# Inverse norms of a delta rule's keys computed apart from those of its queries

## Chip, core and metric

The kernel runs on one core of a Trainium2 chip. A core has five engines that each work through a queue of their own in order: TensorE (PE in the profile, with its weight loads as PEld), VectorE (DVE), ScalarE (ACT), GpSimd (POOL) and SyncE (SP), which here issues nearly all DMA transfers. Semaphores tie the queues together. The metric is device time in microseconds (us), as the median of several runs.

## What is computed

One layer of a hybrid decoder trunk, with 1024 tokens behind 16 meta tokens, width 1024, float32 in and out. A combined input projection feeds two head groups: a gated delta rule (4 heads, key and value width 128) and a forgetting attention (8 heads). Their outputs go through an output projection, then a SwiGLU network, and a last normalisation. The change concerns the delta rule's front, of which this is the part that matters:

```python
def l2norm(x):
    return x * lax.rsqrt(jnp.sum(x * x, axis=-1, keepdims=True) + EPS)

qkv = jax.nn.silu(causal_dwconv(qkv, conv_w))
q, k, v = jnp.split(qkv, ...)
q = l2norm(q) * (GDN_DK ** -0.5)          # per token and head
k = l2norm(k)
# chunks: a_mat = strict(k k^T * decay * beta), qk = q k^T * decay, then
# (I + a_mat) is inverted per chunk and the state is carried from chunk to chunk
```

So each token and head needs two inverse norms: one of its key and one of its query. Keys' inverse norms enter the matrices `a_mat` and `qk` and the keys that update the state; queries' inverse norms scale only the final output of a chunk.

## The kernel before

The kernel runs through stages: normalisation of the input; gates; the delta rule's projections and its preparation per head; the remaining projections (`z`, `fv`, `fk`, `fq`, lines L203 and L615 to L654 among them); the chunk scan; attention; output projection; the SwiGLU network (L1359) and its down projection (L1522). Large products are split into three float32r products.

Heads are prepared in two pairs. For each pair the code projects and convolves keys, queries and values of two heads (`conv_silu`, products at L193 to L195), then calls `gdn_pre` for each head, then `invert_blocks` (L529, L531), a long row of small VectorE instructions on the tile `up` that inverts 32x32 diagonal blocks for both heads together. The second pair's preparation runs beside the first pair's inversion and beside the `z` and `fv` projections on TensorE.

`gdn_pre(h, kq, vt)` does this, in source order:

- L442: fill `stat` with ones. Its columns 0 to 7 (`NT` = 8 token tiles) will hold the sums of squares of the keys, column 8 that of the 16 meta keys, columns 9 to 16 those of the queries (`NS` = 9).
- L445 to L448: transpose the keys (`tr_k`), copy them to `ktok`, square them on ScalarE into `sq`, reduce on VectorE.
- L449 to L454: transpose the meta keys and values (`trm`), copy to `mkv`, square with a sum.
- L455 to L457: transpose the queries (`tr_q`, in two halves), square on ScalarE, reduce on VectorE.
- L458: add EPS to all 18 columns of `stat` in one VectorE instruction.
- L459, L460: two powers of -1/2 on GpSimd, `rk` (keys) and `rq` (queries).
- L461 to L470: transpose `rk` on TensorE (`prk`, L462 and L463), copy to `rkt` (L465, L466), store to DRAM (`rk_d`, L467 and L468), and read it back spread over all partitions as `rkr` (L470).
- L472, L473, L503, L520: small VectorE products with `rk`.
- L477 to L483: load `gc_d` into `gce`, form the decays (L478 and L479 on VectorE, the exponential L480 on ScalarE, two masks L481 and L483 on GpSimd).
- L489 to L496: products of keys with keys and queries (`pq`), and VectorE instructions that multiply them with the decays and with `nbr` or `rk`.
- L498: multiply `na` with `rkr` on GpSimd; L500 stores its diagonal blocks to `ad_d`, which `invert_blocks` reads (L539).
- L504 (GpSimd, `ktok` times `kf`), L507 (values), L509 to L514 (stores to `rec_d`), L517 to L522 (the meta chunk; L518 multiplies `ems` with `rkr`).

`rq` is read again only at L572, behind all heads, and then in the scan. The tiles that `gdn_pre` transposes into come from a pool of three PSUM banks (`ps_t`).

The result of `invert_blocks` goes to DRAM (L549) and is read back as `ubk` (L597) in `levels`, which copies it on ScalarE and VectorE (L606). The gate tiles `zt` are made at L297 (ScalarE) and L298 (GpSimd) and stored at L299.

The order of the queues is not written by hand here. The source is traced in program order, and the framework's scheduler orders each engine's queue at compile time against its own estimate of how long things take:

```python
with tile.TileContext(nc, schedule_with_timeline_sim=True) as tc:
```

Only TensorE has a hand-written order, from the `z` projection on (`peo.enter_context(tc.manual_schedule(...))`); the second pair's TensorE instructions were written ahead of that and stand among them. Once compiled, every queue is fixed.

Of the kernel before, what the change touches and what calls it, by code (L numbers as in the profile page):

```python
# [12 lines left out]
ALU = mybir.AluOpType  # L13
# [8 lines left out]
NT = S // P  # L22
# [5 lines left out]
EPS = 1e-6  # L28
# [69 lines left out]
def tile_hymba_layer(ctx, tc, x, meta, attn_norm_w, w_in, conv_w, a_log, dt_bias, gdn_norm_w,  # L98
                     fgate_b, w_out, ffn_norm_w, w_gate, w_up, w_down, final_norm_w, out):
    nc = tc.nc  # L100
# [20 lines left out]
    def ps_t(name):  # L121
        return bank("tp", 3, name)
# [15 lines left out]
    mhalf = const.tile([P, 32], F32, name="mhalf")  # L138
# [194 lines left out]
    NS = NT + 1  # L333
# [77 lines left out]
    rk = gpool.tile([P, GH, NS], F32, name="rk")  # L411
# [15 lines left out]
    def tr8(src, nm):  # L427
        pts = []
        for g in range(2):
            pt = ps_t(f"tr_{nm}_{g}")  # L430
            for i in range(4):
                c = NM + P * (4 * g + i)
                nc.tensor.transpose(pt[:, P * i:P * i + P], src[:, c:c + P], ident)
            pts.append(pt)
        return pts

    def v3(ap, n=NT):
        return ap.rearrange("p (t c) -> p t c", t=n)

    def gdn_pre(h, kq, vt):  # L440
        stat = gp.tile([P, 2 * NS], F32, tag="kst", bufs=2, name=f"kst_{h}")
# [10 lines left out]
        mkv = gp.tile([NM, 2, P], F32, tag="mkv", bufs=2, name=f"mkv_{h}")  # L452
        nc.scalar.copy(mkv, pt[:NM, 0:2 * P].rearrange("p (a c) -> p a c", a=2))
        nc.scalar.activation(sqq[:NM, :P], mkv[:, 0], AF.Square, accum_out=stat[:NM, NT:NT + 1])  # L454
        for g, pt in enumerate(tr8(kq[:, 1], f"q{h}")):  # L455
            nc.scalar.activation(sqq[:, 512 * g:512 * g + 512], pt, AF.Square)
        nc.vector.tensor_reduce(stat[:, NS:NS + NT], v3(sqq), AX.X, ALU.add)  # L457
        nc.vector.tensor_scalar(stat, stat, EPS, None, op0=ALU.add)  # L458
        nc.gpsimd.tensor_tensor(rk[:, h], stat[:, 0:NS], mhalf[:, :NS], op=ALU.pow)  # L459
        nc.gpsimd.tensor_tensor(rq[:, h], stat[:, NS:NS + NT], mhalf[:, :NT], op=ALU.pow)  # L460
        prk = ps_t(f"prk_{h}")  # L461
        nc.tensor.transpose(prk[:NT, :P], rk[:, h, 0:NT], ident)  # L462
# [22 lines left out]
        for g in range(4):  # L485
# [6 lines left out]
            for i in range(2):  # L492
                t = 2 * g + i
                nc.vector.scalar_tensor_tensor(na[:, t], pqv[:, i, 0], nbr[:, t:t + 1], na[:, t],
                                               op0=ALU.mult, op1=ALU.mult)
                nc.vector.scalar_tensor_tensor(e[:, t], pqv[:, i, 1], rk[:, h, t:t + 1], e[:, t],  # L496
                                               op0=ALU.mult, op1=ALU.mult)
# [53 lines left out]
    for hp in range(2):  # L551
        c = 2 * P * hp
        kqs = [gp.tile([P, 2, T], F32, tag="kq", bufs=3, name=f"kq_{2 * hp + i}") for i in range(2)]
        vts = [gp.tile([P, T], F32, tag="vt", bufs=2, name=f"vt_{2 * hp + i}") for i in range(2)]
        with ExitStack() as es:
            for ins in (xlds[-1], *casts[6]) if not hp else ():
                es.enter_context(tc.issue_after(ins.ins))
            w = win_block(GK + c, 256, f"gk{hp}")
        for i in range(2):
            conv_silu(w, P * i, 4 + 2 * hp + i, kqs[i][:, 0], f"k{hp}{i}")  # L560
        w = win_block(GQ + c, 256, f"gq{hp}")
        for i in range(2):
            conv_silu(w, P * i, 2 * hp + i, kqs[i][:, 1], f"q{hp}{i}")
        w = win_block(GV + c, 256, f"gv{hp}")
        for i in range(2):
            conv_silu(w, P * i, 8 + 2 * hp + i, vts[i], f"v{hp}{i}")
        for i in range(2):
            gdn_pre(2 * hp + i, kqs[i], vts[i])
        invert_blocks(hp)
# [1067 lines left out]
```

## Time and profile before

| what | value |
|---|---|
| median of 3 runs | 1328.59 us (1327.1 to 1329.35) |
| profiled execution, its own time | 1324.81 us |
| its span in the trace | 1323.1 us |
| instructions | 20046 |
| mean granted TensorE clock | 0.997 |
| stage of `gdn_pre` and `invert_blocks`, heads 0 to 3 | about 116 to 272 us of the span |

The profile's page gives busy time per engine over the span; the waits view sums, for an engine, its idle time by what ended it; the timeline lists instructions one by one with start, length and the idle time before them; the windows view gives busy time of each engine and the granted TensorE clock in chosen stretches. "Granted clock" is the share of full speed that the throttle let TensorE have. A SPq row is the issue of a DMA on SyncE's queue, not the transfer.

### The profile page before, as it was taken

What the parts mean: (1) busy time and instruction counts of PE and PEld (TensorE: products, weight loads), DVE (VectorE), ACT (ScalarE), POOL (GpSimd) and SP (SyncE); (2) the same over time, 40 slices, a digit from 0 to 9 for tenths busy, and PEclk for the clock granted to TensorE, in tenths of its full rate; (3) what the DMA queues carried; (4) which work ended last, traced back from release to release, by engine and by line L of the source; (5) the groups of instructions that cost most, each with busy time, mean ns of one, the idle gap of its engine ahead of it and who ended that gap; (6) DMA issues with size and microseconds to landing.
All of it is one profiled execution on the core that took longest, in us unless ns stands there. A gap on an engine that the chain in (4) does not pass through costs nothing.

```text
span 1323.1 us, 20046 instructions
## 1 busy us (share of the span) xinstructions
PE 1296.6 (98%) x7442; PEld 1133.5 (86%) x7442; DVE 851.8 (64%) x1523; ACT 546.3 (41%) x916; POOL 389.3 (29%) x348
## 2 busy tenths in 40 slices
PE   9999999999999999999899999999999999999997
PEld 8999999899999988877687888888888888888886
DVE  6665789676236588885787665566566565355644
ACT  6543534232223367884553333333333243343332
POOL 2211423501023311113422644553334453010301
PEclk9999999999999999999999999999999999999999
DMA  6331743874479596646544555434444557955513
GB/s 228 98 112 33 213 133 117 221 209 146 147 254 332 180 248 184 165 110 211 171 144 134 192 176 183 151 137 159 159 162 157 175 195 259 408 180 185 213 63 127
DMA packets 184776, 233.88 MB, mean 177 GB/s; under 512 B 19120, under 2 KB 136872, under 8 KB 181864
## 3 DMA queue, kind: packets, MB, share of 16 engines
q1 hardware_dynamic: 181704, 223.70, 52.4%
q0 software_dynamic: 2976, 8.92, 2.2%
q8 instruction: 58, 0.95, 0.3%
q14 instruction: 38, 0.31, 0.1%
HBM read 154.91 MB, written 77.67 MB: 176 GB/s over the span
## 4 chain that ended last, share of the span: by engine, by line
PE 82%; DMA 6%; DVE 5%; issue 3%; POOL 2%; ACT 1%; SPq 1%; POOLq 0%; DVEq 0%; ACTq 0%
PE xp L1522 8%; PE yp L1522 7%; PE gb L1359 5%; PE ud L1359 5%; PE gd L1359 5%; PE ub L1359 5%; PE ua L1359 4%; PE ga L1359 4%; PE pj_fk L203 4%; PE pj_fq L203 4%; PE pt L1005 2%; PE ue L1359 2%; PE ge L1359 2%; PE fv L203 2%; PE wog L203 2%
## 5 line engine op out<-in xcount | busy, mean ns | idle before, releaser
L164 DVE TENSOR_TENSOR al_p<-ra_p,ah_p 128x2048 fp32r<-128x2048 f32 (+1 forms) x21 | 46.7, 2222 | 94.0 <-ACT ah_p L163 94.0
L163 ACT CAST ah_p<-ra_p 128x2048 fp32r<-128x2048 f32 (+1 forms) x21 | 37.1, 1766 | 105.8 <-PE xp L1522 48.5
L1522 PE MATMUL xp<-wh_p,ah_p 128*128 128x512 f32 (+1 forms) x187 | 70.5, 377 | 0.7 <-DVE hs L1549 0.7
L1522 PE MATMUL xp<-wl_p,ah_p 128*128 128x512 f32 (+1 forms) x187 | 70.4, 376 | 0.0
L1522 PE MATMUL xp<-wh_p,al_p 128*128 128x512 f32 (+1 forms) x187 | 70.4, 376 | 0.0
L1412 POOL TENSOR_TENSOR gzw<-gzw,uzt 128x512 f32<-128x512 f32 x11 | 18.4, 1675 | 154.0 <-DVE uzt L1403 127.9
L1412 POOL TENSOR_TENSOR gxy<-gxy,uxy 128x512 f32<-128x512 f32 x22 | 38.7, 1758 | 67.0 <-DVE uxy L1403 48.0
L1359 PE MATMUL gb<-uh_p,w_g_p 128*128 128x512 f32 x176 | 57.8, 389 | 0.0
L1359 PE MATMUL ub<-uh_p,w_u_p 128*128 128x512 f32 x176 | 57.8, 389 | 0.0
L1359 PE MATMUL gd<-uh_p,w_g_p 128*128 128x512 f32 x176 | 57.8, 389 | 0.0
L1359 PE MATMUL ud<-uh_p,w_u_p 128*128 128x512 f32 x176 | 57.8, 389 | 0.0
L979 ACT ACTIVATE pr<-pr,sm 128x144 f32<-128x144 f32 (+3 forms) x64 | 50.6, 792 | 16.5 <-DVE sm L974 16.2
L164 DVE TENSOR_TENSOR w_u_p<-raw_u,w_u_p 128x512 fp32r<-128x512 f32 x42 | 43.2, 1028 | 21.4 <-ACT w_u_p L163 21.3
L164 DVE TENSOR_TENSOR pl<-pt,ph 128x512 fp32r<-128x512 f32 (+1 forms) x96 | 51.4, 553 | 4.6 <-ACT ph L163 3.7
L163 ACT CAST ph<-pt 128x512 fp32r<-128x512 f32 (+1 forms) x96 | 45.4, 474 | 17.8 <-PE pt L1005 17.0
L1359 PE MATMUL ga<-uh_p,w_g_p 128*128 128x512 f32 x160 | 52.5, 389 | 0.0
L1359 PE MATMUL ua<-uh_p,w_u_p 128*128 128x512 f32 x160 | 52.5, 389 | 0.0
L1522 PE MATMUL yp<-wh_p,ah_p 128*128 128x512 f32 x132 | 51.3, 389 | 0.0
L1522 PE MATMUL yp<-wl_p,ah_p 128*128 128x512 f32 x132 | 51.3, 389 | 0.0
L1522 PE MATMUL yp<-wh_p,al_p 128*128 128x512 f32 x132 | 51.3, 389 | 0.0
L164 DVE TENSOR_TENSOR wl_p<-rw_p,wh_p 128x2048 fp32r<-128x2048 f32 (+1 forms) x21 | 46.9, 2235 | 3.4 <-ACT wh_p L163 3.4
L1005 PE MATMUL pt<-ident,pr 128*128 128x128 f32 x288 | 48.1, 276 | 0.0
(638 smaller groups left out, 4265.4 us busy)
## 6 DMA issues: line engine op xcount, KB each, us to landing
ra_p<-ao_p SPq DMA_DIRECT2D x14, 1024.0 KB
raw_g<-in_w_gate_dram SPq DMA_DIRECT2D x22, 512.0 KB
raw_u<-in_w_up_dram SPq DMA_DIRECT2D x22, 512.0 KB
raw_d<-in_w_down_dram SPq DMA_DIRECT2D x22, 512.0 KB
wt_p<-raw_d SPq DMA_DIRECT2D x33, 256.0 KB
rw_p<-wt_p SPq DMA_DIRECT2D x8, 1024.0 KB
rw_p<-in_w_down_dram SPq DMA_DIRECT2D x6, 1024.0 KB
ao_p<-gzw SPq DMA_DIRECT2D x22, 256.0 KB
```

The costliest lines, as they stand in the source:

```text
L163: cast = nc.scalar.copy(dst_hi, src)
L164: tail[0] = (cast, nc.vector.tensor_sub(dst_lo, src, dst_hi.bitcast(F32)))
L203: nc.tensor.matmul(dst, a, b, start=first, stop=last)
L979: nc.scalar.activation(pr[:, :n], pr[:, :n], AF.Exp, bias=sm[:, np_ - 1:np_], scale=-1.0, accum_out=rsum[:, h, j:j + 1])
L1005: nc.tensor.transpose(pt[:rows_k, P * j:P * j + P], pts[j][0][:, c0:c0 + rows_k], ident)
L1359: nc.tensor.matmul(dst, a[:, c], b[:, k], start=(first and k == 0 and i == 0), stop=(k == 3 and i == 2), skip_group_check=not first)
L1412: last_mul[0] = G.tensor_tensor(gs[d], gs[d], us[d], op=ALU.mult)
L1522: nc.tensor.matmul(dst[:, n_], a[:, f, c], b[:, f, n_], start=(first and i == 0 and n == 0), stop=(i == NF - 1 and n == 2), skip_group_che ...
```

## The change

In `gdn_pre` the addition of EPS is split in two: columns of the keys (with the meta keys) and columns of the queries. The keys' addition and the keys' power are placed directly behind the meta keys' squares, in front of the queries' transposes and squares. The queries' addition and power stay where they were. The values are the same; the unused column 17 of `stat` no longer gets EPS.

```diff
         nc.scalar.activation(sqq[:NM, :P], mkv[:, 0], AF.Square, accum_out=stat[:NM, NT:NT + 1])
+        nc.vector.tensor_scalar(stat[:, 0:NS], stat[:, 0:NS], EPS, None, op0=ALU.add)
+        nc.gpsimd.tensor_tensor(rk[:, h], stat[:, 0:NS], mhalf[:, :NS], op=ALU.pow)
         for g, pt in enumerate(tr8(kq[:, 1], f"q{h}")):
             nc.scalar.activation(sqq[:, 512 * g:512 * g + 512], pt, AF.Square)
         nc.vector.tensor_reduce(stat[:, NS:NS + NT], v3(sqq), AX.X, ALU.add)
-        nc.vector.tensor_scalar(stat, stat, EPS, None, op0=ALU.add)
-        nc.gpsimd.tensor_tensor(rk[:, h], stat[:, 0:NS], mhalf[:, :NS], op=ALU.pow)
+        nc.vector.tensor_scalar(stat[:, NS:NS + NT], stat[:, NS:NS + NT], EPS, None, op0=ALU.add)
         nc.gpsimd.tensor_tensor(rq[:, h], stat[:, NS:NS + NT], mhalf[:, :NT], op=ALU.pow)
```

## The prediction

> **What bounds the kernel now.** The page comes first: how full is the busiest engine?
>
> ```profile
> PE 1296.6 (98%) x7442; PEld 1133.5 (86%) x7442; DVE 851.8 (64%) x1523; ACT 546.3 (41%) x916; POOL 389.3 (29%) x348
> ```
>
> TensorE has work in 1296.6 of 1323.1 us, so only its idle 26.5 us, and time at a lowered clock, can be won. Next the waits view, cut to TensorE from 110 to 290 us, the stage around the change (engine, line, what it waited for: us, times, longest):
>
> ```profile
> PE prk L462 <- POOL rk L459: 2.1, 1, 2.1
> PE fv L203 <- DVE up L531: 1.1, 1, 1.1
> PE pq L489 <- DVE gce L496: 0.5, 1, 0.5
> PE tr_q L433 <- ACT mkv L453: 0.3, 1, 0.3
> PE pj_v L193 <- ACT cx_q L419: 0.3, 1, 0.3
> ```
>
> The longest is for the very tile that the change moves: the transposes of `rk` (L462) wait 2.1 us for POOL's power (L459), once in four heads. The timeline shows which head (start, length, instruction, idle time before it):
>
> ```profile
> 239.63 0.27 PE L462 MATMUL prk<-ident,rk 128*8 128x128 f32 x1 [2.13 <-POOL rk L459]
> 237.79 1.79 POOL L459 TENSOR_TENSOR rk<-kst,mhalf 128x9 f32<-128x9 f32 x1 [4.20 <-DVE kst L458]
> ```
>
> It is head 3. The windows view, 1 us each, shows what follows (stretch, length, busy time and count of PE, PEld, DVE, ACT, POOL, then granted clock):
>
> ```profile
> 237.00:238.00 1.00, 0.51 (x5) 0.18 (x2) 1.00 (x3) 0.32 (x1) 0.21 (x1) 1.00 0.98 326
> 238.00:239.00 1.00, 0.00 (x0) 0.00 (x0) 1.00 (x2) 0.00 (x0) 1.00 (x1) 1.00 0.15 51
> 239.00:240.00 1.00, 0.36 (x3) 0.21 (x3) 1.00 (x2) 0.54 (x1) 1.00 (x2) 0.90 0.42 56
> 240.00:241.00 1.00, 1.00 (x6) 1.00 (x6) 1.00 (x5) 1.00 (x1) 1.00 (x1) 0.50 0.51 66
> 241.00:242.00 1.00, 1.00 (x7) 1.00 (x6) 1.00 (x2) 1.00 (x3) 1.00 (x1) 0.50 0.51 68
> 242.00:243.00 1.00, 1.00 (x6) 1.00 (x6) 1.00 (x3) 0.58 (x2) 1.00 (x2) 0.50 0.49 63
> 243.00:244.00 1.00, 1.00 (x10) 1.00 (x9) 0.78 (x3) 0.00 (x0) 1.00 (x2) 0.89 0.08 9
> ```
>
> TensorE counts as full from 240, but its clock is halved: 6 or 7 matmuls per us, where the us at 243 has 10. The lost clock is 0.10 + 3 x 0.50 + 0.11 = 1.71 us. The stall costs 2.13 + 1.71 = 3.84 us.
>
> **Why head 3 is late.** VectorE and ScalarE for this head:
>
> ```profile
> 228.03 1.22 DVE L448 TENSOR_REDUCE kst<-sq 128x8 f32<-128x1024 f32 x1 [1.68 <-ACT sq L447]
> 229.17 0.57 DVE L531 TENSOR_REDUCE up<-up 128x14 f32<-128x406 f32 x1
> 229.65 2.10 DVE L518 TENSOR_TENSOR ems<-ems,rkr 16x16 f32<-16x16 f32 x1
> 234.68 1.21 DVE L457 TENSOR_REDUCE kst<-sq 128x8 f32<-128x1024 f32 x1
> 237.54 0.17 DVE L458 TENSOR_SCALAR kst<-kst 128x18 f32<-128x18 f32 x1
> 238.21 1.21 DVE L479 SCALAR_TENSOR_TENSOR gce<-gce 128x1024 f32<-128x1024 f32 x1
> 228.50 0.18 ACT L454 ACTIVATION_READ_ACCUMULATOR sq<-mkv 16x1 f32 x1
> ```
>
> The sums of the keys are complete at 229.25 (L448) and 228.68 (L454), yet the addition of EPS (L458) runs at 237.54, since it takes keys and queries in one instruction and the queries' sums (L457) stand behind other work. That is 8.3 us between the keys' sums and the instruction that uses them.
>
> **The change, part by part.**
>
> 1. Splitting L458. The rows of the two lines over all four heads:
>
> ```profile
> L458 DVE TENSOR_SCALAR kst<-kst x4: 167/168/175, 125.4 to 237.5; 128x18 f32<-128x18 f32 x4
> L459 POOL TENSOR_TENSOR rk<-kst,mhalf x4: 1794/1802/1887, 125.8 to 237.8; 128x9 f32<-128x9 f32 x4
> ```
>
> Four more VectorE instructions of about 0.17 us each: 0.7 us on an engine busy for 64%. I cost them at nothing, because TensorE's stream covers them; uncovered they cost 0.7 us. POOL's powers are the same four and four; nothing is added there, and no DMA is added or taken away.
>
> 2. The keys' addition and power move ahead. POOL at that time:
>
> ```profile
> 229.32 2.40 POOL L498 TENSOR_TENSOR ktna<-ktna,rkr 128x1024 f32<-128x1024 f32 x1 [5.59 <-DVE kst L448]
> 231.66 1.93 POOL L298 TENSOR_TENSOR zt<-zt,gnw 128x256 f32<-128x256 f32 x2
> ```
>
> The addition can run behind L531 at 229.7, or behind L518 at 231.75. The power follows either at once (229.9 to 231.7), or behind L498 (231.7 to 233.5), or last behind both L298 as well (233.6 to 235.4). Against 239.58 now, `rk` is 4.2 to 7.9 us earlier. I take 233.5, behind L498, since head 2's product stands ahead of head 3's power in the source too. L298 then starts 1.8 us later; it feeds a store of the gate that nothing in this stage reads.
>
> 3. TensorE's place for the transposes. If TensorE kept its place (it comes there at 237.5), the stall would be gone: -3.84. But the queues are ordered at compile time against a model of the times, so the transposes will stand earlier too. What the lag can be is shown by the other heads:
>
> ```profile
> 130.90 0.27 PE L462 MATMUL prk<-ident,rk 128*8 128x128 f32 x1
> 125.79 1.81 POOL L459 TENSOR_TENSOR rk<-kst,mhalf 128x9 f32<-128x9 f32 x1
> 215.30 0.27 PE L462 MATMUL prk<-ident,rk 128*8 128x128 f32 x1
> 213.36 1.89 POOL L459 TENSOR_TENSOR rk<-kst,mhalf 128x9 f32<-128x9 f32 x1 [2.19 <-DVE kst L458]
> ```
>
> Head 0 transposes 3.3 us after its power ends (127.60), head 2 just after it (215.25), head 3 stalls. So a new stall between 0 and 2.1 us is what the rows allow. Head 3 differs by what lay on the queries' path: L518 took 2.10 us there (0.17 at 253.47, below) while L498 ran, and it and the steps behind it leave the path. So I take +0.4 us, without loss of clock: gaps of a µs keep it (270 to 272, below).
>
> [...]
>
> 4. What is late next. TensorE would reach its next stall 3.4 us sooner. That is the wait of `fv` at 272:
>
> ```profile
> 272.01 0.36 PE L203 MATMUL fv<-whi_fv,uh 128*128 128x256 f32 x1 [1.12 <-DVE up L531]
> 270.00:272.00 2.00, 0.89 (x8) 0.51 (x7) 1.92 (x8) 1.93 (x4) 0.00 (x0) 1.00 1.17 297
> 269.80 0.62 ACT L606 COPY u<-ubk 32x512 f32<-32x512 f32 x1 [7.14 <-DMA ubk<-ud_d]
> 255.84 2.40 POOL L498 TENSOR_TENSOR ktna<-ktna,rkr 128x1024 f32<-128x1024 f32 x1 [6.49 <-DVE ktna L494]
> 253.47 0.17 DVE L518 TENSOR_TENSOR ems<-ems,rkr 16x16 f32<-16x16 f32 x1 [2.29 <-DMA rkr<-rk_d]
> 246.34 1.20 SPq L470 DMA_DIRECT2D rkr<-rk_d  x1
> 244.44 0.28 SPq L467 DMA_DIRECT2D rk_d<-rkt  x1
> 238.32 3.79 SPq L549 DMA_DIRECT2D ud_d<-up  x8
> ```
>
> Read upwards: `rkt` is stored at 244.44, read back from 246.34, and VectorE waits 2.29 us for it at 253.47; then POOL's L498, SP's stores and loads of the diagonal blocks, and only then ScalarE's L606, in front of which no `fv` bank is evicted. This chain begins at `rk` too. With `rk` 6 us earlier VectorE's 2.29 goes, and POOL has 1.79 us less ahead of head 3's masks: about 4.1 us sooner, against TensorE's 3.4. So the stall of 1.12 us stays nearly as it is: nothing. Bounds: it vanishes, -1.1, or SP's order keeps the chain where it is and the gain is eaten here.
>
> 5. Heads 0 to 2. Each `rk` comes sooner as well, but TensorE is full there apart from 0.5 + 0.3 + 0.3 us in the waits above: nothing, with -1.1 as a bound.
>
> **Sum.** -2.13 - 1.71 + 0.4 + 0 = -3.4 us. The profiled execution took 1324.81 (span 1323.1 and 1.7 around it); it becomes 1321.4. It is 3.8 below the median of the runs, 1328.59, and I put the same difference on that: 1325.2. With everything favourable: -3.84 - 1.1 - 1.1 = -6.0, 1322.6.
>
> **The rivals.**
>
> *The gain is given back at `fv`.* If the chain of part 4 stays put, TensorE stands there for 1.1 + 3.8 = 4.9 us and restarts at half clock for another 1.7: 1328.6 to 1330.3. If the chain comes 2 us sooner: -2 + 1.7, 1328.3. For it: SP issues in order, and the eight stores of the inversion (L549, until 242.1, the last row above) may stand ahead of the read-back. Against it: VectorE's wait at 253.47 is for `rk` alone.
>
> *The wait moves along with the transposes, and is longer there: slower.* Place: head 3, on TensorE, behind the queries' transposes at about 229. POOL's L498 must wait for its DMA until 229.32, so a power queued behind it ends at 233.5. The queries' transposes end at 229:
>
> ```profile
> 228.31 0.66 PE L433 MATMUL tr_q<-ident,kq 128*128 128x128 f32 x4 [0.28 <-ACT mkv L453]
> ```
>
> If TensorE comes to L462 at 230, it idles 3.5 us, not 2.1; at 228.7, 4.8 us. With the same 1.7 of clock that is +1.4 to +2.7: 1330.0 to 1331.3. It decides from the point at which TensorE comes more than 2.1 us before the power's end. Against it: in three heads of four it came behind.
>
> *The clock is not won back.* [...] If the halved clock at 240 has another cause than the gap of 2.13 us, 1.71 drops out: -2.13 + 0.4 = -1.7, 1326.9. The windows speak against it: the clock falls inside the gap and nowhere else near, though 1.12 us at 272 cost nothing.
>
> [...]
>
> *The change doesn't do what it says.* If the addition or the power is queued as late as now, 1328.6.
>
> **Chances.** A measurement of this kernel tells about 0.2% (2.7 us) from no change. Forecast 0.50 (faster 0.46, same 0.04); given back at `fv` 0.16 (0.02 faster, 0.11 same, 0.03 slower); the wait moves and grows 0.17 (0.02 same, 0.15 slower); the clock stays lost 0.05 (same); VectorE held up 0.02 (same); no effect 0.10 (0.02 faster, 0.07 same, 0.01 slower). Sums: faster 0.50, same 0.31, slower 0.19. The range goes from the favourable sum, 1322.6, to 1331.3, the far end of the slower rival; the forecast's own is 1322.6 to 1327.
>
> **What would show it.** Right: in head 3 `rk` starts by 234 and far ahead of L457; no idle time of 2 us before L462; clock 1.00 from 236 to 246; the second `rkr` of the pair issued by 243; a stall of about 1 us for `fv` near 268. Wrong: a gap of 2 us before L462 at an earlier time with half clock behind it, a gap of 3 us or more before `fv`, or L459 still behind L457.

## The result, and the profile after

The changed kernel takes 1340.09 us (median of 4 runs, 1339.09 to 1341.11); before, beside it, 1327.84 us (4 runs, 1326.06 to 1329.35). The ratio is 1.0095, interval 1.0073 to 1.0117: **slower by 0.95%**, where 0.25% faster was forecast, and outside the range. Timed again later on another occasion, 6 runs gave 1339.01 us against 1330.68, ratio 1.006 (1.0038 to 1.0082). The profiled execution took 1341.11 us, its span is 1339.0. Ratios here and below leave out two single executions that took far longer: one of e9's at 4532.11 us, which e9's median in the table counts, and one of before's at 2592.77 us, beside e5 to e8.

Line numbers of the changed kernel are one higher than before's behind the moved lines: the keys' addition and power are L455 and L456, the transposes of `rk` L463 and L464, `rkt` L466 and L467, `rkr` L471.

The page's busy times come first:

```profile
PE 1305.1 (97%) x7442; PEld 1139.3 (85%) x7442; DVE 850.7 (64%) x1527; ACT 548.4 (41%) x918; POOL 391.8 (29%) x348
```

TensorE has the same 7442 instructions but is busy 8.5 us longer (1296.6 before): it did the same work at a lower clock, 0.992 granted on average against 0.997. Its idle time grew as well. The waits view of TensorE from 110 to 345 us (engine, line, what it waited for: us, times, longest):

```profile
PE prk L463 <- POOL rk L456: 3.0, 3, 1.8
PE pq L490 <- DVE gce L497: 1.8, 1, 1.8
PE pj_v L193 <- ACT cx_q L419: 1.7, 1, 1.7
PE py L641 <- DVE u L631: 1.2, 1, 1.2
PE fv_-1_3081 L203 <- DVE up L532: 0.7, 1, 0.7
PE py L643 <- DVE u L631: 0.6, 1, 0.6
PE fv L203 <- DVE up L532: 0.4, 1, 0.4
PE trm L451 <- ACT vt L425: 0.3, 1, 0.3
```

That is 9.7 us in eight rows; before it was 4.3 in five. The wait for `rk` that the change was to remove is still the largest. It is now spread over three places instead of one, and `cx_q`, `py` and a second `fv` have come in, none of which is a wait for `rk`.

Where was the most lost? The windows view, 3 us each, of the levels behind the heads (length, busy time and count of PE, PEld, DVE, ACT, POOL, granted clock):

```profile
315.00:318.00 3.00, 2.27 (x18) 1.93 (x14) 2.61 (x7) 1.70 (x3) 0.00 (x0) 1.00 0.05 16
318.00:321.00 3.00, 1.91 (x23) 1.59 (x24) 2.87 (x7) 0.58 (x1) 0.00 (x0) 0.95 0.02 5
321.00:324.00 3.00, 3.00 (x17) 2.39 (x15) 0.59 (x2) 0.58 (x1) 0.09 (x1) 0.50 0.35 121
...
333.00:336.00 3.00, 3.00 (x12) 3.00 (x12) 0.52 (x1) 0.41 (x1) 0.97 (x1) 0.50 0.38 126
336.00:339.00 3.00, 3.00 (x16) 3.00 (x15) 0.00 (x0) 0.00 (x1) 0.00 (x0) 0.71 0.34 112
```

TensorE is idle for 0.73 + 1.09 us, and then runs for 17 us at half clock (five whole windows at 0.50 and parts of two): 0.15 + 7.50 + 0.87 = 8.5 us of clock. The same place in before has no such gap, nor have the windows behind it:

```profile
311.00:314.00 3.00, 3.00 (x30) 2.53 (x29) 2.51 (x6) 1.63 (x4) 0.00 (x0) 1.00 0.27 82
```

The timeline names the cause of that gap. After:

```profile
315.27 0.71 DVE L601 STREAM_TRANSPOSE tb<-ubk 128x512 f32<-128x512 f32 x1 [4.11 <-DMA ubk<-ud_d]
...
317.76 0.67 DVE L631 COPY u<-pu 32x512 f32<-32x512 f32 x1
318.49 0.41 PE L641 MATMUL py<-ident,u 64*64 64x64 f32 x4 [1.22 <-DVE u L631]
```

VectorE stood for 4.11 us at the second pair's transposition (it waits for that pair's `ubk`), while the first pair's copies (L631) stood behind it; the last matmul that they wait for ended at 315.2. Before, the two had the other order:

```profile
310.44 1.40 DVE L630 COPY u<-pu 32x512 f32<-32x512 f32 x2 [1.31 <-PE pu L626]
312.54 0.71 DVE L600 STREAM_TRANSPOSE tb<-ubk 128x512 f32<-128x512 f32 x1 [0.40 <-DMA ubk<-ud_d]
```

Nothing in the diff touches this place. The scheduler put VectorE's queue into another order there, and not only there: the tables of queue order that e5, e10 and e12 (below) carry hold another instruction at 452 places of TensorE's queue, 309 of VectorE's, 97 of SP's, 44 of ScalarE's and 23 of POOL's, from the heads to the levels.

The ledger closes up to the scan. The scan behind the levels starts, in the tile view of `sc` (min, median and longest ns, first and last start):

```profile
L971 PE MATMUL sc<-ka,qa x112: 230/368/447, 458.4 to 592.7; 70*128 70x264 f32 x16, 70*128 70x328 f32 x16, 70*128 70x392 f32 x16, 70*128 70x456 f32 x16
```

and after the change

```profile
L972 PE MATMUL sc<-ka,qa x112: 230/368/448, 472.4 to 607.0; 70*128 70x264 f32 x16, 70*128 70x328 f32 x16, 70*128 70x392 f32 x16, 70*128 70x456 f32 x16
```

It starts 14.0 us later, of the 15.9 by which the span grew. More idle time, 9.7 - 4.3 = 5.4, and 8.5 of clock in the levels are 13.9. The half clock behind head 3 (1.7 in the prediction) went, and as much came back behind the wait for `pq` at 248 (0.75, 0.50 and 0.89 in the three stretches of 2 us from 248).

Not every execution loses its clock at the same place. Each run states the mean granted clock of its span, so (1 - clock) x span is the time it lost to the clock. Before loses 4.0 to 4.5 us on average, with 1325.3 to 1326.0 left; the changed kernel lost 11.7 (first 4 runs) and 9.1 (6 runs later), with 1328.4 and 1330.0 left. So of its loss some 6 us are clock and some 4 us idle time. In the profile of the second occasion the levels kept their clock (0.6 us of waits for `u`), and 2.5 us of waiting for `fv` at 268 and others cost it instead.

### The profile page after: what moved, and what is told of

It reads as the page before. It is cut to its first block, busy times and chain, and to the rows that moved or that the text cites. A ratio compares the mean times of both kernels' runs of the same rounds, so it can differ in the third digit from the quotient of the medians.

```text
span 1339.0 us, 20058 instructions
## 1 busy us (share of the span) xinstructions
PE 1305.1 (97%) x7442; PEld 1139.3 (85%) x7442; DVE 850.7 (64%) x1527; ACT 548.4 (41%) x918; POOL 391.8 (29%) x348
## 4 chain that ended last, share of the span: by engine, by line
PE 76%; DVE 10%; DMA 6%; issue 3%; POOL 2%; ACT 1%; SPq 1%; POOLq 0%; DVEq 0%; ACTq 0%
PE xp L1523 8%; PE yp L1523 7%; PE gb L1360 4%; PE ud L1360 4%; PE gd L1360 4%; PE ub L1360 4%; PE ua L1360 4%; PE ga L1360 4%; PE pj_fq L203 4%; PE pj_fk L203 3%; PE pt L1006 2%; PE ue L1360 2%; PE ge L1360 2%; PE wog L203 2%; DMA of<-o_d 2%
```

## The experiments

Ratios are against before, timed beside each run; line numbers in rows of an experiment are its own, a few higher than before's:

| run | what | median us | ratio (interval) |
|---|---|---|---|
| e1 | changed kernel, levels' order on VectorE restored | 1338.25 | 1.0054 (1.0031 to 1.0077) |
| e2 | before, with the changed kernel's order there | 1337.24 | 1.0054 (1.0033 to 1.0074) |
| e3 | change in head 3 alone, levels' order restored | 1343.0 | 1.0077 (1.005 to 1.0104) |
| e4 | change in heads 0 to 2, levels' order restored | 1332.83 | 1.0024 (1.0009 to 1.0039) |
| e5 | split alone, all queues held as before | 1330.23 | 1.0007 (0.9991 to 1.0023) |
| e6 | head 3, all queues held as before | 1327.43 | 0.9988 (0.9977 to 0.9999) |
| e7 | all heads, all queues held as before | 1327.99 | 0.9995 (0.9984 to 1.0006) |
| e8 | split alone, `rk` late, queues free | 1333.26 | 1.004 (1.0027 to 1.0054) |
| e9 | e6, `rkt` copied ahead of the casts | 1329.06 | 0.9989 (0.9974 to 1.0004) |
| e10 | changed kernel, the levels' gap filled | 1339.0 | 1.0053 (1.0034 to 1.0071) |
| e11 | changed kernel again | 1339.01 | 1.006 (1.0038 to 1.0082) |
| e12 | changed kernel, TensorE's queue as before | 1341.35 | 1.0089 (1.0071 to 1.0107) |
| e13 | e9, with more of head 3's chain ahead | 1331.79 | 1.0016 (1.0003 to 1.0029) |
| e14 | e13's places, `rk` late | 1332.59 | 1.0021 (1.001 to 1.0031) |

**The levels' order (e1 and e2).** e1 queues the second pair's transposition behind the first pair's copies; it differs from the changed kernel in that alone:

```diff
-        V.transpose(tb.rearrange("p h t c -> p (h t c)"), ubk.rearrange("p h t c -> p (h t c)"))
+        with tc.issue_after(lv_cp[-1].ins) if lv_cp else nullcontext():
+            V.transpose(tb.rearrange("p h t c -> p (h t c)"), ubk.rearrange("p h t c -> p (h t c)"))
...
-            V.tensor_copy(u[r, :, :, q], py[r])
+            lv_cp.append(V.tensor_copy(u[r, :, :, q], py[r]))
```

e2 does the reverse to before (the second pair's levels are offered as early as the first's, and the copies queued behind the transposition):

```diff
-            V.tensor_copy(u[r, :, :, q], py[r])
+            with tc.issue_after(lv_tr[1].ins) if not hp else nullcontext():
+                V.tensor_copy(u[r, :, :, q], py[r])
...
-        od.add(levels(hp), LV0[hp] - 8.0)
+        od.add(levels(hp), LV0[0] - 8.0)
```

> The changed kernel, with one order pinned on VectorE: the second pair's transposition of ubk is queued behind the first pair's two copies into u. Nothing else in any queue differs. Theory Q (in the changed kernel VectorE waits 4.1 us for the second pair's ubk with the first pair's copies queued behind it; TensorE then idles 1.8 us and runs at half clock for 17 us, 10 us in all): about 1330, and a granted clock of 1.00 from 318 to 338. Rival G (the time is lost in the stage of the four heads, the clock there included, and the later gap only shifts): 1337 to 1340.

> The kernel before, with the one order reversed: the first pair's two copies into u are queued on VectorE behind the second pair's transposition of ubk. Theory Q: ubk lands at about 312.5, so the copies end near 315.4 in place of 311.8, TensorE idles some 3 us from 312.4 and then runs at half clock for about 17 us: 1328 + 3 + 8 = about 1339. If the half clock has another cause than this gap: 1331. Rival G: 1328.

e2's profile shows the damage made to order: the wait and, in the windows view, the half clock behind it.

```profile
PE py L643 <- DVE u L633: 2.0, 1, 2.0
```

```profile
319.00:322.00 3.00, 3.00 (x20) 2.21 (x20) 1.62 (x5) 1.16 (x2) 0.00 (x0) 0.50 0.35 124
...
331.00:334.00 3.00, 3.00 (x15) 2.88 (x15) 0.94 (x2) 0.46 (x1) 1.05 (x1) 0.50 0.28 87
```

So that edit is enough to make before 0.54% slower. But e1, without it, is still 0.54% slower than before. Its waits from 110 to 345 us have no `py` any more; the two longest are

```profile
PE fv L203 <- DVE up L532: 2.7, 1, 2.7
PE prk L463 <- POOL rk L456: 2.6, 3, 1.8
```

The levels are not the whole of the loss. How large a part they are e1 leaves open, since its interval overlaps those of the changed kernel on both occasions.

**Which heads (e3 and e4).** The change for some heads only (`early = h in (3,)` or `(0, 1, 2)`; the others keep the joint addition), with e1's order in the levels:

```diff
+        early = h in (3,)
+        if early:
+            nc.vector.tensor_scalar(stat[:, 0:NS], stat[:, 0:NS], EPS, None, op0=ALU.add)
+            nc.gpsimd.tensor_tensor(rk[:, h], stat[:, 0:NS], mhalf[:, :NS], op=ALU.pow)
```

> The split for head 3 alone (heads 0 to 2 keep the joint addition), with the order of e1 pinned. The prediction's mechanism by itself: no wait of 2.1 us before the transposes of rk of head 3, clock 1.00 from 236 to 246, about 3.4 us faster than before: 1324.5. Rival (the transposes move along with the power and wait as long as before): 1328. Rival (the gain is given back at the wait of fv): 1328 to 1330.

> The split for heads 0 to 2 alone, with the order of e1 pinned. Theory Q plus a loss of some 2 us in the heads' stage (waits of 1.7 us for cx_q and 1.8 us for rk of head 2, which the profile of the changed kernel shows): about 1330, with these two waits seen again. Rival (these waits come from head 3 or from chance): 1328.

Head 3 alone, the head with all of the forecast gain, came out 0.77% slower: four of its 6 executions took 1342.89 to 1344.73 us and two 1334.43 and 1334.49. The profile is of one of these two:

```profile
PE prk L469 <- POOL rk L458: 2.0, 1, 2.0
PE fv L203 <- DVE fr L887: 1.8, 2, 1.6
```

The wait for `rk` is as long as before, only sooner (the last transposes of `rk` start at 235.0, not 239.8): the scheduler moved the transposes with the power. Heads 0 to 2 cost 0.24%. Each version was put into an order of its own, so parts of the change cannot be added up this way, and the next runs hold the order.

**The order held (e5 to e8).** In e5 to e7 each engine's queue is tied, instruction by instruction, to the order of before. The table lists, for each engine, which traced instruction stands where; a negative number is a new addition:

```diff
+    for e, runs in order.items():
+        at = [n for a, m in runs for n in (range(a, a + m) if a >= 0 else [a])]
+        stand = [new[-1 - n] if n < 0 else traced[e][n] for n in at]
+        for x, y in zip(stand, stand[1:]):
+            tc.add_manual_dep(y, x.name, mybir.DependencyInfo(mybir.DependencyClass.NoSync, mybir.DependencyReason.DATA),
+                              reason="order")
```

An edge of this kind orders two instructions of one queue and waits for nothing. In the traces of e5 to e7 the rows of TensorE and of SP stand in the order of before, one for one. e5 splits the addition and leaves both halves where the joint one stood; e6 moves the keys' addition and power of head 3 alone, and e7 those of all heads. e8 also only splits, ties the keys' addition behind the queries' sums so that `rk` is as late as in before, and leaves the queues free:

```diff
-        nc.vector.tensor_reduce(stat[:, NS:NS + NT], v3(sqq), AX.X, ALU.add)
+        qred = nc.vector.tensor_reduce(stat[:, NS:NS + NT], v3(sqq), AX.X, ALU.add)
+        with tc.issue_after(qred.ins):
+            nc.vector.tensor_scalar(stat[:, 0:NS], stat[:, 0:NS], EPS, None, op0=ALU.add)
```

> The split alone: two additions of EPS per head instead of one, the power at its old place, and the queues of all five engines held in the order of the kernel before by issue edges (the four more additions of 0.17 us are the only difference in any queue). Theory A, the loss comes from the order into which the queues fell: 1.000 of before within 0.1%, about 1329.4, with the wait of 2.1 us for rk in head 3 and the half clock behind it still there. Theory B, the four more instructions or the waits that come with them cost something themselves: above 1331.5.

> The change for head 3 alone: its keys' addition stands on VectorE behind the reduction of 229.2 (L531), its power on POOL behind the product of 229.3 (L498); everything else of all five queues, TensorE's transposes of rk among it, is held in the order of before. Theory A (order): this is what the prediction priced, so prk has no wait, the clock stays at 1.00 from 236 to 246, and the time is 2 to 4 us below before, 1325.4 to 1327.4 against 1329.4. Theory C, the early power holds up VectorE or the saving is given back at fv: prk has no wait, but fv or pq wait 2 us or more longer, and the time is within 1 us of before.

> The change for all four heads as above, each power on POOL as soon as its sums allow, all other places in the queues held as before. Theory A: as the run before within 1 us, 1325 to 1328, since heads 0 to 2 have no wait for rk in before. [...]

> The split with the keys' addition tied behind the queries' sums, so rk is as late as in before, and no queue held: the compiler's scheduler places everything. Its queues differ from before in 137 rows of TensorE and 166 of VectorE, though nothing is ready earlier. Theory A (the order that a scheduler falls into is what costs, not the early rk): 3 to 8 us above before, 1332 to 1337, with new waits of TensorE between 110 and 320 us. Theory D, the loss needs the early rk: within 1.5 us of before.

This settles the main question. e7 has the changed kernel's instructions and its dependencies; only the places in the queues differ. It takes 1327.99 us where the changed kernel takes 1339 to 1340. The edges themselves are not what makes it fast: e10 (below) holds the changed kernel's own queues by the same edges and takes 1339.0. e7's trace has some long rows (keys' additions of up to 2.23 us, a power of 2.78), but they cost no time that can be told from noise. And e8, in which the keys' addition still waits for the queries' sums (its last power starts at 237.7, before's at 237.8), is 0.4% slower, with waits that before does not have or has shorter:

```profile
PE prk L464 <- POOL rk L461: 4.3, 2, 2.9
PE fv L203 <- DVE fr L879: 2.4, 1, 2.4
PE pj_v L193 <- ACT cx_q L419: 2.1, 1, 2.1
```

**The early `rk` is not what costs; the order into which the queues fell is.** The split itself costs nothing that can be measured (e5). e8's order is not the changed kernel's: it shows that another order can cost by itself, not how much each place of this one does.

e6 is the prediction's own sum put to the test, with TensorE keeping its place. Its longest wait, and the stretches behind it:

```profile
PE pm L520 <- DVE rkt L469: 1.7, 1, 1.7
```

```profile
245.00:246.00 1.00, 1.00 (x6) 1.00 (x6) 1.00 (x2) 0.28 (x1) 1.00 (x1) 0.50 1.04 286
...
247.00:248.00 1.00, 1.00 (x6) 1.00 (x6) 0.96 (x4) 0.00 (x0) 1.00 (x4) 0.50 1.10 293
```

The waits for `rk` and for `fv` are gone; the others are 0.7 us or less. But 1.7 us come back at `pm`, and with them 3 us of half clock. For that case part 3 of the prediction gives -3.84 us; the ratio of 0.9988 leaves -1.6 us (-3.1 to -0.1), and the medians are 2.2 us apart.

**Following the wait (e9, e13, e14).** `pm` waits because VectorE's copies of the transposed `rk` (`rkt`) stand behind two casts. e9 puts them ahead. e13 then moves POOL's two masks ahead of its product for `ktok`, VectorE's two instructions for `mkv` behind head 3's products, and SP's stores of `ktok` and `mkv` behind that of `nam`; e14 has the same places with `rk` late. The edits are in the table of the order (numbers are traced instructions, by their line in before):

```diff
 VectorE (e9, e13):
   L479,
+  L465, L466,
   L164, L472, L473, L503, L164,
-  L465, L466,
   L508,
 POOL (e13):
+  L481, L483,
   L504, L572,
-  L481,
   L541, L573,
-  L483,
```

> The run for head 3 alone in the old queues (e6), with one more place changed: VectorE's two copies of rk's transposes (rkt) stand ahead of the two low parts of raw_fv (L164, 1.22 and 1.21 us), behind the scalar_tensor_tensor of 238.84. In e6 TensorE waited 1.71 us for these copies ahead of pm at 243.45, and ran 3 us at half clock behind it. Theory A, what was won at rk came back at rkt because VectorE's order was made for a later rk: the wait at pm goes, the clock stays at 1.00 from 240 to 252, and the time is 2 to 3.5 us below e6 and 4 to 6 us below before. Rival, another wait steps in again (pq, fv or cx_q): a new gap of 1 us or more between 240 and 275 us, and the time within 1 us of e6.

> As e9 (head 3's rk early, rkt ahead of the casts, all else in the old queues), with the next step of head 3's chain moved too: POOL's two masks of the exponentials ahead of its product for ktok (L507, which took 3.96 us in e9 beside VectorE's casts), VectorE's two instructions for mkv behind head 3's products, and SP's stores of ktok and mkv behind the one of nam. In e9 TensorE waited 2.7 us for pq, whose bank VectorE freed late because the mask came behind L507. Theory A, the gain is passed from reader to reader until the whole chain is moved: waits from 225 to 300 us below 1.5 us in all, no halved clock there, 1323 to 1326 against 1330 before. Rival, some gap of 1 us or more always steps in because TensorE's order leaves it nothing else to do at that place: within 1.5 us of e6 (0.9988 of before).

> The same places in all queues as e13, but head 3's rk where it was in before (addition and power behind the queries' sums): the control for e13. Theory A: TensorE waits about 2.1 us for rk again with half clock behind it; 2 to 4 us above e13. Rival, what e13 wins comes from the masks and rkt alone: the same time as e13 within 1 us.

In e9 the wait for `pm` is gone and `pq` has it, longer:

```profile
PE pq L492 <- DVE gce L499: 3.3, 2, 2.7
```

```profile
245.80 3.96 POOL L507 TENSOR_TENSOR ktna<-ktna,kf 128x1024 f32<-128x1024 f32 x1 [0.26 <-DVE kf L506]
...
250.21 1.09 POOL L484 TENSOR_SCALAR_AFFINE_SELECT ktna<-gce 128x1024 f32<-128x1024 f32 x1
```

The mask that `pq`'s readers need stands behind a product of 3.96 us on POOL. e13 takes that away, and the wait is at `fv`, longer still, where ScalarE stands 7.48 us for `ubk`:

```profile
PE fv L203 <- DVE up L534: 4.2, 1, 4.2
```

```profile
270.60 0.62 ACT L609 COPY u<-ubk 32x512 f32<-32x512 f32 x1 [7.48 <-DMA ubk<-ud_d]
```

With `rk` late in the same places (e14) TensorE waits 2.0 us for `rk` and 2.8 for `fv`, and the time is the same within the intervals: the medians are 0.8 us apart, so in these places an early `rk` wins nothing clear of noise. The rival written beside e9 was right; e13 is slower than either theory had it, and the gap that steps in is the longest of the three. ScalarE's copy waits for the read-back `ubk`; what holds that back was not tested.

**Clock or idle time in the levels (e10, e11).** 14 transposes of the identity stand on TensorE ahead of L641, and the changed kernel's queues are held otherwise:

```diff
+            for _ in range(14 if not hp and not t2s else 0):
+                fills.append(nc.tensor.transpose(bank2[:, 0:P], ident, ident))
             for t in range(4):
                 nc.tensor.transpose(p2[lo, 0, t], u[lo, i, t0 + t, lo], ident[lo, lo])
```

> The changed kernel with its own queues held as they are, and 14 transposes of the identity (128x128, about 0.14 us each, 1.9 us together) put on TensorE directly ahead of the first transposes of u (L641), where it idles 1.2 us and then 0.6 us in the levels. Their results are overwritten and used by nothing. They take away no wait, they only keep TensorE at work in it. Theory A, the loss in the levels is the halved clock over 17 us and not the idle time: the clock stays at 1.00 from 315 to 340, 6 to 8 us of the changed kernel's loss come back, 1331 to 1335. Rival, the matmuls there are slow for another reason (their operands' arrival, the copies behind them): the clock may stay up but the time stays at 1338 or more.

> The changed kernel once more, beside the two others on the same chip: 1339 to 1341 us, with half clock from 321 to 336 us in the profiled execution. If half clock there is a matter of chance, single executions lie near 1332.

The levels kept their clock in e10:

```profile
322.00:325.00 3.00, 3.00 (x35) 2.40 (x34) 0.15 (x1) 1.16 (x2) 0.00 (x0) 1.00 0.38 124
325.00:328.00 3.00, 3.00 (x33) 2.31 (x33) 0.96 (x3) 0.58 (x1) 1.62 (x2) 1.00 0.14 42
```

In such a window the changed kernel's first profile had 17 to 24 matmuls. Yet the median did not move: 1339.0 against 1339.01 for e11. So the rival's time came, though not by its reason. In e11's profile the same order leaves a gap of only 0.6 us there, and the clock stays full, though none of its 6 executions came below 1335.37. And e10's executions lost 7.6 us of clock on average, e11's 9.1: in e10's profile 1.7 us each went at 16, 218, 272 and 378 us instead, among others. Half clock in the levels cost 8.5 us in the profile where it struck; it does not carry the loss alone.

**TensorE's queue alone (e12).** The table holds TensorE's queue in the order of before and the other four in that of the changed kernel; in short:

```diff
-    order = {"PE": <changed>, "DVE": <changed>, "Activation": <changed>, "Pool": <changed>, "SP": <changed>}
+    order = {"PE": <before>,  "DVE": <changed>, "Activation": <changed>, "Pool": <changed>, "SP": <changed>}
```

> The changed kernel (all four heads' rk early) with TensorE's queue alone held in the order of the kernel before; the queues of VectorE, ScalarE, POOL and SP stand as in the changed kernel. The run e7 holds all five in the old order and took 1328.0; the changed kernel, with the same instructions and the same dependencies, 1339. Theory P, the loss lies in where TensorE's instructions stand (transposes of rk and of the queries taken too early): 1326 to 1331 here. Theory Q, it lies in the order of the engines that serve TensorE (VectorE's copies and casts, SP's transfers): 1336 or more, with waits for fv, pq and u as in the changed kernel. Between the two: both have a part.

It is among the slowest, and TensorE never waits for `rk` in it. Its three longest waits:

```profile
PE fv L203 <- ACT zt L297: 5.6, 1, 5.6
PE pj_q L193 <- ACT cx_k L419: 3.0, 1, 3.0
PE fv L203 <- DVE up L534: 2.8, 1, 2.8
```

The time is the second theory's, but the two longest are not the changed kernel's waits. So the loss is not in TensorE's places alone. It does not follow that it lies in the other four: an old queue against four new ones makes waits that neither kernel has (5.6 us for `zt`). A queue is good or bad with the others. How the changed kernel's loss divides among single waits stays open.

## Why the prediction was wrong, step by step

1. *The split costs nothing.* Not contradicted: e5, 1.0007 (0.9991 to 1.0023), an interval wider than the 0.7 us at stake.

2. *`rk` 4.2 to 7.9 us earlier, power from 231.7 to 233.5.* Right. In the profile after:

```profile
229.23 2.39 POOL L499 TENSOR_TENSOR ktna<-ktna,rkr 128x1024 f32<-128x1024 f32 x1 [4.00 <-DMA rkr<-rk_d]
229.84 1.80 DVE L455 TENSOR_SCALAR kst<-kst 128x9 f32<-128x9 f32 x1
231.72 2.10 POOL L456 TENSOR_TENSOR rk<-kst,mhalf 128x9 f32<-128x9 f32 x1
233.88 0.27 PE L463 MATMUL prk<-ident,rk 128*8 128x128 f32 x1 [1.02 <-POOL rk L456]
```

`rk` is complete at 233.82, 5.8 us earlier than before. The steps up to here are not what failed.

3. *The wait and the half clock go; +0.4 us for the transposes' new place.* **Here it failed.** I let the queues react to the early `rk` with one instruction, the transposes, and bounded that at 0 to 2.1 us in head 3. The scheduler re-sorted everything from the heads to the levels. In head 3 the wait is 1.0 us (last row above) and its clock is kept, which is near what I took; but head 2 now waits 1.8 us where it waited none, and in all the wait for `rk` is 3.0 us instead of 2.1.

4. *What is late next: `fv`, in step with TensorE.* Wrong. In the changed kernel the second `rkr` of the pair was to be issued by 243:

```profile
241.11 1.24 SPq L468 DMA_DIRECT2D rk_d<-rkt  x1
242.44 5.32 SPq L550 DMA_DIRECT2D ud_d<-up  x8
247.79 0.30 SPq L469 DMA_DIRECT2D rk_d<-rkt  x1
...
249.29 1.05 SPq L471 DMA_DIRECT2D rkr<-rk_d  x1
```

It was issued at 249.29, 3 us *later* than before (246.34), although `rk` came 5.8 us earlier: the eight stores of the inversion, which before stood ahead of both stores of `rkt`, now stand between them. The prediction's first rival named these stores as what could stand in the way. With the queues held, the next stall was not `fv` either but `pm` behind `rkt`, 5 us behind the transposes (e6): VectorE's copies had not moved, and I had followed the chain through `rkr` without asking who else needs the bank of `prk`. Only when `rkt` and the mask had been moved did the wait reach `fv`, 4.2 us with half clock behind it (e13); the rival had priced it at 4.9.

5. *Heads 0 to 2: nothing, and nothing behind head 3.* Wrong by the same omission: `cx_q` at 186 (1.7 us), head 2's `rk` (1.8), the levels' gap (1.8, and 8.5 of clock in the profiled execution).

Of the sum, -2.13 - 1.71 + 0.4, the wait and the half clock of the first two terms did go, but with the queues held only 1.6 to 2.2 us of them were kept (e6), since the wait returned at `pm` with half clock. The term +0.4 stood for the scheduler's answer, and it is the one that was mis-sized: as measured, that answer is 9 to 13 us, the changed kernel's 1.006 and 1.0095 against e7's 0.9995.

Of the rivals, the slower one (the wait moves along and grows in head 3) had the right sign and the right motion of the transposes, but not the size, 1.4 to 2.7 us, nor the place. That its sign came true is luck. The chance for *VectorE held up* did not come true: in head 3 VectorE's four rows beside the power (231.72 to 233.82) took 0.62 to 0.64 us each. The reverse was seen, in head 1: a power beside a VectorE row that had started 0.13 us earlier (L423, 143.04 to 144.34) took 2.83 us instead of 1.8. And in head 3 it was POOL's product, not its power, beside which a VectorE row was long: L455 ran from 229.84 to 231.64, beside POOL's product L499 (229.23 to 231.62), 1.80 us for an addition whose median is 0.17:

```profile
L455 DVE TENSOR_SCALAR kst<-kst x4: 161/166/1802, 123.5 to 229.8; 128x9 f32<-128x9 f32 x4
```

## What to carry to other kernels

Where a compile-time scheduler orders the queues, an edit that makes a value ready earlier need not move one instruction only: compare the order of all queues first, and price the stage as a new one. To learn what an edit is worth by itself, hold the queues in their old order and let only the edited instructions move; here that turned a loss of 0.6 to 0.95% into no difference (e7), and for head 3 alone into a gain of 0.12% (e6). A wait removed on the way of one buffer can come back at the next reader of the same chain (`rk`, `rkt`, `pq`, `fv` here), so follow every reader of the tile, not the one with the longest latency.

## What the runs showed that was not expected

A wait of TensorE did not always cost its clock. The same wait ahead of `pm` did in e6 (1.71 us) and did not in e7 (1.66 us); in the profile after, 1.8 us at `pq` did and 1.7 us at `cx_q` did not; in e9 even 2.7 us at `pq` did not. Here are e6's gap, which is followed by half clock (above), then e7's, then e9's with the stretches behind it:

```profile
241.00:242.00 1.00, 0.74 (x7) 0.53 (x5) 1.00 (x5) 1.00 (x2) 0.80 (x1) 1.00 0.50 66
242.00:243.00 1.00, 0.00 (x0) 0.00 (x0) 1.00 (x1) 1.00 (x4) 0.94 (x1) 1.00 0.51 67
243.00:244.00 1.00, 0.55 (x5) 0.52 (x6) 1.00 (x4) 0.21 (x1) 1.00 (x1) 1.00 0.62 130
244.00:245.00 1.00, 1.00 (x10) 1.00 (x10) 1.00 (x1) 0.09 (x1) 0.91 (x2) 0.91 0.19 62
```

```profile
244.00:248.00 4.00, 2.34 (x20) 2.10 (x20) 4.00 (x7) 2.24 (x5) 3.65 (x3) 1.00 0.52 102
248.00:252.00 4.00, 4.00 (x35) 4.00 (x34) 3.44 (x11) 0.38 (x1) 3.78 (x7) 1.00 1.12 269
```

```profile
250.00:252.00 2.00, 1.30 (x11) 1.09 (x9) 0.90 (x4) 0.00 (x0) 1.93 (x5) 1.00 1.05 282
252.00:254.00 2.00, 0.02 (x1) 0.02 (x1) 1.30 (x6) 0.00 (x0) 1.21 (x3) 1.00 1.08 233
254.00:256.00 2.00, 2.00 (x12) 1.82 (x12) 1.10 (x5) 0.00 (x0) 0.00 (x0) 1.00 0.92 307
256.00:258.00 2.00, 2.00 (x17) 1.97 (x16) 1.48 (x7) 0.00 (x0) 0.00 (x0) 1.00 1.10 325
```

Behind e6's gap of 1.71 us 0.09 + 3 x 0.50 + 0.11 = 1.70 us of clock are lost, behind e9's of 2.7 none. So the length of a gap alone did not decide here whether the clock fell; what did was not tested. Nor did executions of one kernel pay at the same places: the profile after lost 1.7 us of clock from 248 and 8.5 in the levels, e11's, of the same kernel, 1.7 us each near 218, 272, 484 and 620.

The prediction took half clock as a fixed price of a gap of 2 us, and read the clock as falling inside the gap. Its window at 239 (0.90) puts the fall at 239.8, behind the gap's end at 239.63.

How long half clock lasted differed too: 3.4 us in e6, where `fv`'s products on the full array follow, and 17 us in the levels, where products on a 64x64 part of it run between the others until 332 (the profile after; in e2 the clock lost there is 8.5 us as well). In e13 the stretch behind the wait for `fv` cost 3.4 us of clock. And in e4 from 372 us and e10 from 376, 1.7 us of clock went although TensorE was busy for all of the 4 us windows around. Whether the kind of product matters was not tested.
